# Seven products for eight in the mixer's input projection, with sums made by adding DMAs

## The chip, the cores and the metric

The kernel runs on one core of a Trainium2 chip. The metric is the device time of one execution in microseconds (us). Before the change three runs took 2020.88 to 2021.68 us, median 2021.68. Engines are named as in the profile: PE (TensorE, the matmuls), PEld (its weight loads), DVE (VectorE), ACT (ScalarE), POOL (GpSimd), SP (SyncE, which only issues DMAs here).

## The reference

One layer of a streaming encoder over T = 576 frames (512 of a prompt, 64 of a sample), width 1024, all in float32:

```
h = x + 0.5 * swiglu(rmsnorm(x), w_ffn1)          # 1024 -> 2 x 4096 -> 1024
h = h + mixer(rmsnorm(h))
h = h + 0.5 * swiglu(rmsnorm(h), w_ffn2);  y = rmsnorm(h)

mixer(u):  z, xbc, dt, aq, ak, av, mq, mk, mv, mo, mi, mf, gl = split(u @ w_in)
  y_ssd  = rmsnorm(ssd_scan(silu(conv4(xbc)), dt) * silu(z))      # 16 heads x 64, state 128
  y_att  = chunk-band softmax attention(aq, ak, av)               # 8 heads x 64
  y_ml   = rmsnorm(mlstm_scan(mq, mk, mv, mi, mf)) * sigmoid(mo)  # 4 heads x 128
  g_ssd, g_att, g_ml = split(sigmoid(gl))
  out = (g_ssd * (y_ssd @ w_proj_ssd) + g_att * (y_att @ w_proj_attn) + g_ml * (y_ml @ w_proj_mlstm)) @ w_out
```

Caches and states are inputs, and the new ones are outputs too. The input projection `u @ w_in` has 1024 rows and some 9,700 columns; it is the largest product of the mixer.

## The kernel before

Activations lie transposed in SBUF: 128 channels on the partitions, 8 channel slices, 576 frames along the free dimension. A float32 product is made from three fast ones: each operand is split into a rounded part (`wh`, `XH`, float32r, an ACT copy) and the rest (`wl`, `XL`, a DVE subtraction), and hi*hi + hi*lo + lo*hi are summed in PSUM.

A plain column tile (`gemm`, `matmuls`, L183) is 128 columns of a weight: a 512 KB load, one split of 128x1024 (L169, L170), and for each of the two frame ranges of 256 and 320 columns 8 slices x 3 = 24 matmuls. Its result goes through PSUM to `evac`, a DVE multiplication by the norm's factor `rs`.

The two FFNs already use another scheme for most of their first product (`swiglu_unit`, L404): two column tiles, two halves of the 1024 rows and two frame ranges of 288 form a 2x2 by 2x2 product, made in 7 products in place of 8 (`product`, L396, matmuls at L401). `operands` (L353) makes the seven moving operands `TH`, `TL` once per norm; `stationary` (L372) loads 1 MB of weights, adds them on POOL (L380 to L382) and splits seven blocks of 128x512. Each product is 4 x 3 = 12 matmuls of 288 columns. Three PSUM banks `pa`, `pb`, `pc` hold a unit.

The mixer runs twelve units in the order a0 a1 m0 a2 m1 m2 a3 m3 s0 s1 s2 s3 (a: two attention heads, 3 column tiles; m: one mLSTM head, 4 tiles; s: one SSD group of four heads, 6 tiles: z0, z1, B, C, x0, x1). Each unit's tiles are projected from `XH`, `XL`, and then the unit's own work runs on all engines: scores, softmax, transposes and products for attention (L616 to L689), `ml` (L708), the scan for SSD (`ssd`, L841 to L951). A `gate` tile feeds `gates` (L505), whose rows mLSTM and SSD need. Attention and mLSTM outputs are split into `YH`, `YL`; SSD outputs stay in `R1`.

`merge` (L954) then makes, for each of 4 column pairs, the sigmoid gates from `w_in`, the projections of attention and mLSTM, then the norm of the SSD outputs, the SSD gates and projection, and `w_out` (L1003 to L1010). The residual x waits in DRAM (`xs`) meanwhile.

Buffers are tiles from pools: a tag has a fixed number of buffers, and a new tile of a tag waits for the readers of the one whose place it takes; a pool opened after another was closed takes over its memory with the same kind of wait. In the mixer `g` (7) holds projected tiles, `t` (5) and `b` (6) a unit's larger temporaries, `P` (3) and `Q` (2) smaller ones. A planner places the program's instructions in each engine's queue by its own estimate of their times; each engine then works through its queue in order. SP issues nearly all DMAs, in the planner's order too.

## Time and profile before

| | us |
|---|---|
| median of three runs | 2021.68 |
| the profiled execution | 2022.94 |
| its span | 2021.2 |
| PE busy | 1968.9 |
| DVE busy | 1224.0 |
| ACT busy | 819.1 |
| POOL busy | 594.7 |

The profile is one execution. A row of groups gives line, engine, operation, tiles (out<-in), shapes and count, then total busy time in us, the mean in ns of one, and the idle time before with what ended it. A row of the timeline gives start and length in us. A row of stages gives a stretch, its length, busy time of PE, PEld, DVE, ACT and POOL with counts in brackets, the granted share of the PE clock, the share of DMA time and GB/s. Matmuls overlap, so that a row's duration is longer than the distance to the next.

In time the kernel runs FFN1 up to 608, the mixer's projections, attention and mLSTM up to about 950, SSD up to 1146, the merge and `w_out` up to 1415, then FFN2.

### The profile page before, as it was taken

To read this page: it belongs to the slowest core of one execution; us is meant where nothing else is said; L and a number is where in the kernel's file an instruction comes from. 1 tells how busy PE (TensorE), PEld (TensorE's weight loads), DVE (VectorE), ACT (ScalarE), POOL (GpSimd) and SP (SyncE) were. 2 spreads that over 40 slices of the span, in tenths; PEclk is the share of its full clock that TensorE was granted. 3 is DMA by queue.
4 is the path that set the end of the run, shared out by engine and by line. 5 is a ranking of instruction groups with operands and counts; after the bars stand their busy time and mean duration, and the time that the engine had idled before them with its cause. 6 is when DMAs were issued, how large, how long until landed. Compare 5 with 4: busy or idle time off the path is not lost.

```text
span 2021.2 us, 35535 instructions
## 1 busy us (share of the span) xinstructions
PE 1968.9 (97%) x14573; PEld 1916.4 (95%) x14573; DVE 1224.0 (61%) x2122; ACT 819.1 (41%) x1474; POOL 594.7 (29%) x564
## 2 busy tenths in 40 slices
PE   7899999999998999999999999999899999999997
PEld 7799999999997888989999999999799999999997
DVE  7865665656546856565777534444876566656554
ACT  3444334434433355454445323233453443344343
POOL 4443332433301010202343401330252343324221
PEclk8899999999998999999999999999899999999998
DMA  2221222232224322222333222321122213222221
GB/s 101 94 105 67 101 99 72 92 109 90 74 87 150 111 88 72 101 65 76 107 106 108 71 84 84 131 74 63 49 109 94 105 63 105 95 73 95 97 85 65
DMA packets 54778, 182.85 MB, mean 90 GB/s; under 512 B 5824, under 2 KB 17728, under 8 KB 47064
## 3 DMA queue, kind: packets, MB, share of 16 engines
q1 hardware_dynamic: 53640, 179.44, 25.5%
q8 instruction: 115, 1.88, 0.4%
q10 hardware_dynamic: 976, 1.14, 0.2%
q14 instruction: 47, 0.39, 0.1%
HBM read 171.80 MB, written 8.76 MB: 89 GB/s over the span
## 4 chain that ended last, share of the span: by engine, by line
PE 93%; DVE 3%; DMA 1%; issue 1%; POOL 1%; ACT 0%; POOLq 0%; SPq 0%; DVEq 0%; ACTq 0%
PE acc L183 55%; PE acc L401 31%; PE ps_s L652 1%; PE ps_v L663 1%; PE ps_x L640 1%; DMA w<-in_wblk 1%; PE ps_s L919 1%; PE ps_v L939 0%; DVE YL L261 0%; PE ps_x L945 0%; DVE YL L213 0%; PE ps_x L610 0%; DVE vl L213 0%; DVE TL L213 0%; DVE sq L297 0%
## 5 line engine op out<-in xcount | busy, mean ns | idle before, releaser
L183 PE MATMUL acc<-YH,wh 128*128 128x256 f32 (+1 forms) x1472 | 440.3, 300 | 14.4 <-ACT wh L169 14.4
L183 PE MATMUL acc<-YL,wh 128*128 128x256 f32 (+1 forms) x1472 | 440.2, 299 | 2.8 <-DVE YL L261 2.5
L183 PE MATMUL acc<-YH,wl 128*128 128x256 f32 (+1 forms) x1472 | 438.0, 300 | 3.7 <-DVE wl L170 3.7
L183 PE MATMUL acc<-XH,wh 128*128 128x256 f32 (+1 forms) x1360 | 407.9, 300 | 6.8 <-ACT wh L169 6.8
L183 PE MATMUL acc<-XH,wl 128*128 128x256 f32 (+1 forms) x1360 | 407.5, 300 | 2.5 <-DVE wl L170 2.5
L183 PE MATMUL acc<-XL,wh 128*128 128x256 f32 (+1 forms) x1360 | 408.8, 301 | 0.0
L169 ACT CAST wh<-w 128x1024 fp32r<-128x1024 f32 x177 | 185.6, 1048 | 292.3 <-PE acc L183 225.5
L183 PEld LDWEIGHTS acc<-YH,wh 128*128 128x128 f32 x1472 | 282.9, 192 | 15.2 <-ACT wh L169 15.0
L183 PEld LDWEIGHTS acc<-YL,wh 128*128 128x128 f32 x1472 | 283.7, 193 | 3.8 <-DVE YL L261 3.7
L183 PEld LDWEIGHTS acc<-YH,wl 128*128 128x128 f32 x1472 | 280.6, 192 | 5.4 <-DVE wl L170 5.2
L401 PE MATMUL acc<-TH,wh 128*128 128x288 f32 x928 | 274.2, 296 | 0.0
L401 PE MATMUL acc<-TL,wh 128*128 128x288 f32 x928 | 273.5, 295 | 0.0
L401 PE MATMUL acc<-TH,wl 128*128 128x288 f32 x928 | 271.6, 295 | 1.9 <-DVE wl L213 1.9
L183 PEld LDWEIGHTS acc<-XH,wh 128*128 128x128 f32 x1360 | 257.3, 189 | 13.7 <-ACT wh L169 7.4
L183 PEld LDWEIGHTS acc<-XH,wl 128*128 128x128 f32 x1360 | 257.1, 189 | 7.8 <-issue 4.7
L183 PEld LDWEIGHTS acc<-XL,wh 128*128 128x128 f32 x1360 | 257.4, 189 | 5.9 <-issue 5.4
L170 DVE TENSOR_TENSOR wl<-w,wh 128x1024 fp32r<-128x1024 f32 x177 | 224.5, 1269 | 61.2 <-ACT wh L169 61.2
L380 POOL TENSOR_TENSOR sm<-w 128x1024 f32<-128x1024 f32 x58 | 141.0, 2432 | 327.0 <-DVE vl L213 136.3
L401 PE MATMUL acc<-TH,vh 128*128 128x288 f32 x696 | 206.1, 296 | 1.7 <-ACT vh L212 1.7
L401 PE MATMUL acc<-TH,vl 128*128 128x288 f32 x696 | 205.3, 296 | 1.9 <-DVE vl L213 1.9
L401 PE MATMUL acc<-TL,vh 128*128 128x288 f32 x696 | 205.7, 296 | 0.0
L466 DVE SCALAR_TENSOR_TENSOR R<-acc,R 128x256 f32<-128x256 f32 (+1 forms) x256 | 115.1, 454 | 117.4 <-PE acc L183 116.2
(302 smaller groups left out, 3363.2 us busy)
## 6 DMA issues: line engine op xcount, KB each, us to landing
w<-in_wblk SPq DMA_DIRECT2D x177, 512.0 KB, 3.3
w<-in_sblk SPq DMA_DIRECT2D x58, 1024.0 KB, 4.9
b<-scr_rows SPq DMA_DIRECT2D x24, 288.0 KB, 4.2
b<-scr_rows SPq DMA_DIRECT2D x16, 144.0 KB, 3.3
R<-xs SPq DMA_DIRECT2D x1, 2304.0 KB
R<-in_xT SPq DMA_DIRECT2D x2, 640.0 KB, 7.9
xs<-R SPq DMA_DIRECT2D x4, 320.0 KB, 3.3
out_y<-R SPq DMA_DIRECT2D x2, 640.0 KB, 3.2
```

What stands on the lines that cost most here:

```text
L169: nc.scalar.copy(hi, w)
L170: nc.vector.tensor_tensor(lo, w, hi.bitcast(F32), op=ALU.subtract)
L183: nc.tensor.matmul(ps[:, :n], wt[:, wsl], xx[:, k0 + k, a:a + n], start=(k == 0 and i == 0), stop=(k == nk - 1 and i == 2))
L380: nc.gpsimd.tensor_tensor(s[:, 0:2, :], w[:, 0:2, :], w[:, 1:3, :], op=ALU.add)
L401: self.nc.tensor.matmul(ps, wt[:, wsl], xx[:, t, kk, :], start=(start and kk == 0 and i == 0), stop=(kk == 3 and i == 2), skip_group_check ...
L466: nc.vector.scalar_tensor_tensor(x[:, ot, sl], ps, 0.5, x[:, ot, sl], op0=ALU.mult, op1=ALU.add)
L640: nc.tensor.transpose(pt[:L, k:k + 128], P[:, k0 + k:k0 + k + L], self.ident)
L652: nc.tensor.matmul(ss[r][:, :nk], q[H[r], c * 128:(c + 1) * 128], kT[H[r], :nk], start=True, stop=True)
L663: nc.tensor.matmul(pv[H[r], c * 128:(c + 1) * 128], vt[:, k, H[r]], PT[r][:, k, :], start=(k == 0), stop=(k == c))
L919: nc.tensor.matmul(ps[:, :128], bt[:n, c, :], xw[:n, c, :], start=True, stop=True)
```

## The change

The mixer's 76 column tiles of `w_in` are regrouped. The six tiles of a0 and a1 and the gate tile stay plain. The other 70 become 35 pairs, each in seven products:

- `operands` is called four times during the plain tiles, so that `TH`, `TL` (now allocated for the whole kernel) hold the mixer's normalised input. They already contain `rs`, so that evacuations only scale.
- `pair` is the new unit: seven `product` calls, four ACT copies or activations from PSUM, three DVE evacuations, two of them with a sum.
- `stationary_fine` gets a pair's weights in pieces of 128x512: three loads (`wr`, 5 buffers), two sums made by DMA (`added`: a load on SP's queue into `wx`, 3 buffers, and a second DMA on POOL's queue that adds to it), and two sums made by POOL (`wy`, 2 buffers). Seven splits of 128x512 go to `ph`, `pl` (6 buffers). Plain tiles in the mixer are loaded and split in halves the same way.
- Three PSUM banks serve both forms in turn.

To make room, branch outputs go to DRAM (`ys`, 16 rows of 128x576) as they are made. `XH`, `XL` exist only for the plain tiles; `P`, `Q`, `t`, `bias` then take their memory, and after the last SSD unit `YH`, `YL` take it in turn, filled from `ys` by loads and splits. `b` is now six slices of `R1`; z of every SSD unit is in `R1` slices 0 and 1, and the unit's tile order is B, C, x0, x1, z0, z1. The squares for the SSD norm are summed at each unit's end. `merged` is `R1` itself, and `XH`, `XL` for `w_out` lie over `TH`, `TL`; x comes back by four DMAs after that. The order of units is a0 a1 m0 a2 a3 m1 m2 m3 s0 to s3; `g` has 8 buffers. In the FFN phases `YH`, `YL` move from the constant pool into the phase's own pool, and the squares of the first norm share one buffer.

The core of the diff:

```diff
-NB = 177
-NS = 58
+NB = 107
+NS = 93
-BUFS = {"g": 7, "b": 6, "t": 5, "P": 3, "Q": 2}
+BUFS = {"g": 8, "t": 5, "P": 3, "Q": 2}
...
+    def stationary_fine(self, src):
+        nc = self.nc
+        def load(q):
+            w = self.ring("wr")
+            nc.sync.dma_start(w, src[:, q, :])
+            return w
+        def added(q0, q1):
+            x = self.ring("wx")
+            nc.sync.dma_start(x, src[:, q0, :])
+            nc.gpsimd.dma_start(x, src[:, q1, :], accum_op=ALU.add)
+            return x
+        out = {}
+        x1 = added(0, 1)
+        a11, a22 = load(0), load(2)
+        x3 = self.ring("wy")
+        nc.gpsimd.tensor_tensor(x3, x1, a22, op=ALU.add)
+        out[self.T_X1] = self.parts(x1)
+        out[self.T_A11] = self.parts(a11)
+        a21 = load(3)
+        x2 = added(1, 2)
+        x4 = self.ring("wy")
+        nc.gpsimd.tensor_tensor(x4, x3, a21, op=ALU.add)
...
+    def pair(self, one, two):
...
+        self.product(pa, ops, self.T_X1, True)
+        v = tmp()
+        nc.scalar.activation(v, pa, AF.Copy, scale=s1)
+        self.product(pb, ops, self.T_A11, True)
+        put1(1, H[1], emit(pb, s1, v, ALU.add))
+        self.product(pa, ops, self.T_X3, False)
+        u = tmp()
+        nc.scalar.activation(u, pa, AF.Copy, scale=s2)
+        self.product(pc, ops, self.T_X4, True)
+        m6 = tmp()
+        nc.scalar.activation(m6, pc, AF.Copy, scale=s2)
+        self.product(pa, ops, self.T_A22, False)
+        put2(0, H[0], emit(pa, -s2, m6, ALU.add))
+        self.product(pc, ops, self.T_A21, False)
+        put2(1, H[1], emit(pc, s2, u, ALU.subtract))
+        self.product(pa, ops, self.T_X2, False)
+        put1(0, H[0], emit(pa, s1))
...
-        self.split(y, self.YH[:, i, :], self.YL[:, i, :])
+        nc.sync.dma_start(self.ys[i], y)
...
+        gates(O_GA, 0)
+        gates(O_GM, 0)
+        with self.pools("my", "yp"):
+            self.YH = self.yp.tile([128, 8, T], F32R, name="YH")
...
+            for i in range(8):
+                self.split(load(i), self.YH[:, i, :], self.YL[:, i, :])
...
+                tiles = [t for u in ORDER[:2] for t in got[u][0]]
+                self.plain(tiles[:3], half_major=True)
+                for n, t in enumerate(tiles[3:]):
+                    self.operands(x, self.rs, C_GM, n)
+                    self.plain([t])
+                self.operands(x, self.rs, C_GM, 3)
```

## The prediction

> **What bounds the kernel now.** I read the page's first part, then the chain of waits, then the matmuls in order of time, then the busy time by stages.

> ```profile
> span 2021.2 us, 35535 instructions
> PE 1968.9 (97%) x14573; PEld 1916.4 (95%) x14573; DVE 1224.0 (61%) x2122; ACT 819.1 (41%) x1474; POOL 594.7 (29%) x564
> PE 93%; DVE 3%; DMA 1%; issue 1%; POOL 1%; ACT 0%; POOLq 0%; SPq 0%; DVEq 0%; ACTq 0%
> ```

> PE sets the end: 93% of the chain. Its busy time says nothing of the price of one matmul, since neighbours overlap; that is the distance between starts:

> ```profile
> 304.98 0.30 PE L401 MATMUL acc<-TH,wh 128*128 128x288 f32 x1
> 306.58 0.30 PE L401 MATMUL acc<-TH,vh 128*128 128x288 f32 x1
> ...
> 1204.82 0.28 PE L183 MATMUL acc<-XH,wh 128*128 128x256 f32 x1
> 1207.65 0.31 PE L183 MATMUL acc<-XH,wh 128*128 128x320 f32 x1
> 1208.38 0.31 PE L183 MATMUL acc<-XH,wl 128*128 128x320 f32 x1
> ```

> Twelve matmuls of 288 columns take 1.60 us (0.1333 each), 24 of 256 take 2.83 (0.118), five of 320 take 0.73 (0.146). A plain column tile, 24 + 24 matmuls, costs PE 24 x 0.118 + 24 x 0.146 = 6.33 us; two cost 12.66. A unit of seven products is 84 matmuls of 288: 11.20 us.

> Stages: plain tiles at the mixer's start; attention and mLSTM; three ssd units; the ssd tail; merge; w_out; the start of FFN2.

> ```profile
> 613.70:664.00 50.30, 46.14 (x314) 43.95 (x315) 32.16 (x64) 16.11 (x29) 6.54 (x13) 0.89 0.33 116
> 664.00:958.00 294.00, 294.00 (x2136) 259.71 (x2135) 179.48 (x453) 138.18 (x313) 39.74 (x83) 1.00 0.26 85
> 958.00:1110.00 152.00, 152.00 (x1188) 145.63 (x1187) 113.47 (x279) 68.94 (x133) 61.63 (x108) 1.00 0.34 110
> 1110.00:1146.00 36.00, 36.00 (x290) 34.33 (x291) 20.61 (x47) 9.88 (x17) 18.40 (x23) 1.00 0.21 71
> 1146.00:1366.00 220.00, 220.00 (x1660) 219.78 (x1660) 101.07 (x157) 68.25 (x117) 45.49 (x49) 1.00 0.27 93
> 1416.00:1485.00 69.00, 57.09 (x373) 54.51 (x374) 56.07 (x75) 30.12 (x46) 22.69 (x15) 0.90 0.21 77
> ```

> Columns: length, then PE, PEld, DVE, ACT and POOL busy, the granted clock, the DMA share. PE has no hole from 664 to 1366; DVE is at 61% in attention and mLSTM, 75% in ssd, 46% in the merge. So time saved on PE counts, until DVE, which pays for the new scheme, has no room.

> **The change, part by part.**

> *Saving.* 70 column tiles become 35 pairs: 35 x (12.66 - 11.20) = **-51.1 us** on PE. All else is what this sets loose.

> *What a pair asks of the other engines.*

> ```profile
> L170 DVE TENSOR_TENSOR wl<-w,wh 128x1024 fp32r<-128x1024 f32 x177 | 224.5, 1269 | 61.2 <-ACT wh L169 61.2
> L213 DVE TENSOR_TENSOR vl<-w,vh 128x512 fp32r<-128x512 f32 x58 | 61.4, 1059 | 1.0
> L212 ACT CAST vh<-sm 128x512 fp32r<-128x512 f32 x116 | 72.3, 623 | 160.1 <-POOL sm L380 155.3 <-PE acc L401 4.8
> L420 ACT COPY P<-acc 128x288 f32<-128x288 f32 x58 | 22.8, 393 | 2.2 <-PE acc L401 2.2
> L427 DVE TENSOR_TENSOR P<-P,acc 128x288 f32<-128x288 f32 x58 | 26.3, 453 | 122.4 <-PE acc L401 122.3
> L699 DVE SCALAR_TENSOR_TENSOR g<-acc,rs 128x320 f32<-128x320 f32 x16 | 7.8, 486 | 6.5 <-PE acc L183 6.4
> L811 DVE TENSOR_TENSOR P<-acc,rs 128x256 f32<-128x256 f32 x16 | 6.7, 416 | 1.4 <-PE acc L183 1.4
> L213 DVE TENSOR_TENSOR YL<-g,YH 128x576 fp32r<-128x576 f32 x68 | 57.8, 850 | 13.3 <-ACT YH L212 13.1
> L223 DVE TENSOR_TENSOR na<-na,sq 128x256 f32<-128x256 f32 x27 | 12.0, 444 | 2.9 <-ACT sq L222 2.2
> ...
> 305.70 0.69 DVE L213 TENSOR_TENSOR vl<-w,vh 128x512 fp32r<-128x512 f32 x1
> ...
> 314.63 1.23 DVE L213 TENSOR_TENSOR vl<-sm,vh 128x512 fp32r<-128x512 f32 x1
> ...
> 314.01 1.29 POOL L381 TENSOR_TENSOR sm<-sm,w 128x512 f32<-128x512 f32 x1
> ```

> Two plain tiles cost DVE 2 x 1.27 (splits) + 2 x (0.42 + 0.49) (evacuations) = 4.36 us. A pair costs 7 splits of 512 and 3 evacuations of 288: 7 x 0.69 + 3 x 0.45 = 6.2 us with POOL still, and 7 x 1.06 + 1.4 = 8.8 at the mean of the second row. The last two rows show why: the split at 314.63 begins while a POOL add runs (314.01 to 315.30) and takes 1.23 for 0.69. Each pair brings two POOL adds of 512 and two DMAs issued by POOL. [...]

> *ssd.* A unit takes 152/3 = 50.7 us: DVE 37.8, ACT 23.0, POOL 20.5. DVE loses 6 x 1.27 of splits and about 6.0 of evacuations, and gains 21 x 0.69 = 14.5, twelve or so evacuations (4.6, the conv's being in pieces) and four adds of squares (1.8): +7.3, less about 1 for the 0.06 by which neighbours overlap. Six adds of 1.3 us on POOL, met half the time at half their length or more, give about +3. DVE: 47. ACT: 23 + 21 x 0.62 - 6 x 1.05 + 12 x 0.39 + 1.7 = 36. PE: 50.7 - 3 x 1.46 = 46.3. Two engines are full; neither packs perfectly in order, so I take 48: four units, **+7** above the PE figure. Bounds: 0, and at 1.06 a split 37.8 - 13.6 + 22.3 + 6.4 = 52.9, or +26.

> *Attention and mLSTM.* Eleven pairs bring DVE 11 x about 3 us, less the eight splits of outputs that move to the merge (0.85 each): 179.5 + 26 in 294 - 16 = 278, 74%. No price for that; the merge (12 pairs in 220 us) has more room still.

> *Operands of the pairs.* Four calls in the plain stage, at the rows of the FFN's:

> ```profile
> L359 DVE SCALAR_TENSOR_TENSOR xk<-R,cst,rs 128x576 f32<-128x576 f32 x16 | 14.1, 925 | 3.0 <-ACT rs L277 3.0
> L363 DVE TENSOR_TENSOR xd<-xk 128x576 f32<-128x576 f32 x8 | 7.2, 902 | 0.1
> L213 DVE TENSOR_TENSOR TL<-xd,TH 128x1440 fp32r<-128x1440 f32 x8 | 13.2, 1653 | 1.7 <-ACT TH L212 1.7
> L213 DVE TENSOR_TENSOR TL<-xk,TH 128x576 fp32r<-128x576 f32 x8 | 5.9, 749 | 0.0
> ```

> 2 x 0.93 + 2.5 x 0.9 + 1.65 + 0.75 = 6.5, four times 26 us. DVE's 32.2 becomes 58 in 50.3; some of the 32.2 belongs to attention, which now comes later. **+5** before the first pair; bounds 0 and 12.

> *Attention starts later.* P, Q, t lie where XH and XL were, so unit a0 waits for the gate tile's last matmul, about 664:

> ```profile
> 649.54 0.60 PE L610 MATMUL ps_x<-ident,g 128*128 128x128 f32 x4
> ...
> 704.03 0.23 DVE L688 COPY t<-ps_v 128x64 f32<-128x64 f32 x1 [0.74 <-PE ps_v L687]
> ```

> It took 54 us, under which PE had plain tiles. Now a0 and a1 hold six of the eight g buffers, and one m0 pair (11.2 us) fits before a0 returns some. **+8**, nearer to the low end because vT and q are freed well before the unit ends; bounds 0 and 25 (40 us of attention less that pair and its own matmuls).

> *The ssd tail.* The projections need YH and YL, which now lie on the branch buffers and come back from DRAM once ssd(3) is through:

> ```profile
> 1103.71 0.80 DVE L822 SCALAR_TENSOR_TENSOR g<-P,cst,g 128x579 f32<-128x579 f32 x1
> ...
> 1145.31 0.30 POOL L951 TENSOR_TENSOR R<-g,R 128x64 f32<-128x64 f32 x1
> ```

> 41 us from the last conv to the end, and some 6 for squares, their total and four split slices: 47. Cover on PE: the z pair (now last) 11.2, two gate pairs 22.4, ssd's own matmuls 50.7 - 6 x 6.33 = 12.7: 46. **+4**; bounds 0 and 15 (the z pair, whose R1 slots unit s2 frees late, as cover for nothing).

> *Ends of the mixer.* FFN's YH and YL move into its pool, on top of the mixer's weight rings, so their norm can't run beside the last w_out matmuls, and the mixer's first weights wait for FFN1's:

> ```profile
> 613.72 0.58 PE L183 MATMUL acc<-XH,wh 128*128 128x256 f32 x1 [5.18 <-ACT wh L169]
> ...
> 1419.79 0.74 PE L237 MATMUL ps_x<-ones,na 128*128 128x1 f32 x4 [4.57 <-DVE na L223]
> ```

> Both places stand idle about 5 us already. **+5** for FFN2 (eight adds and splits of 0.44 and 0.5 are 7.5; bounds 0 and 9), **+2** for FFN1's end and the shared squares buffer at the start (0 and 6).

> *Sums by DMA.* A pair's X1 is a load and an adding load behind it. No row has an adding DMA; the nearest are

> ```profile
> w<-in_wblk SPq DMA_DIRECT2D x177, 512.0 KB, 3.3
> w<-in_sblk SPq DMA_DIRECT2D x58, 1024.0 KB, 4.9
> ```

> so 6.6 to 10 us for both, against three buffers for two sums per pair, 1.5 pairs or 17 us ahead. POOL waits for the first to land before it issues the second, and the x3 add is queued behind. **+2**; bounds 0 and 35 x 1.5 = 52 (a POOL add of 1.5 ahead of each).

> Sum: -51.1 + 7 + 5 + 8 + 4 + 5 + 2 + 2 = -18.1. The profiled execution took 2022.94 (its span 2021.2 and 1.7 around it): 2004.8. The median of the runs, 2021.68, lies 1.3 below: **2003.5 us**.

> **The rivals.**

> *DVE becomes the bound (slower).* Place: attention to ssd; price: splits at 1.06 behind POOL's adds. ssd +26 for +7; 77 splits of 0.37 more in attention, half of it on the path, +14; a0, chained through the same queue, at its bound, +17. 2003.5 + 50 = 2053. It decides against the change once an ssd unit passes 50.7. For: the 1059 row. Against: 61% and 46% around it, and FFN units that run without holes at that mean.

> *PE stays full (faster).* The planner fills every hole but the ends: -51.1 + 9 = -42, 1980. For: no hole from 664 to 1366 now. Against: the g buffers.

> *The pairs don't cost 11.2 (no gain).* X1 late behind POOL, 0.7 us a pair: +25 less the 2 above, 2026. For: POOL's 20 of 50 us in ssd. Against: the 17 us ahead.

> *Holes halve the clock.* Holes of 5.18, 1.67 and 2.48 us stand before the 613.70 row's 0.89, and 0.90 stands at 1416; 11% of 50 us is 5.5 lost, beyond the hole. Three new holes (a0, hand-over, tail) at 3.5: +10, 2013.5. [...]

> **How the numbers follow.** Forecast 0.36, DVE bound 0.26, PE full 0.17, no gain 0.11, clock 0.10. 0.2% (4 us) is about what a measurement can tell from no change. Faster: 0.33 + 0.17 + 0.09 + 0.03 = 0.62; slower: 0.23 + 0.06 + 0.01 = 0.30; same: 0.08. The forecast's own range is 1990 to 2018. The range for 8 in 10 takes in the no-gain case, half of the full-PE case and half of the DVE case: 1982 to 2046.

> **What would show it.** Starts of 288-column matmuls 0.133 apart in the mixer; a unit of ssd near 48 us with DVE above 90%; a PE hole around 670 to 700 ended by attention, another before the first projection ended by DVE YL. Wrong if those holes are absent, if waits on the splits stand between products throughout, or if X1's products wait for DMA.

## The result and the profile after

The changed kernel takes **2075.65 us** (median of four runs, 2073.32 to 2079.95) against 2021.68 (2020.88 to 2021.98) on the same chip: **1.027 times** the time before, 95% interval 1.0252 to 1.0288. The forecast was 2003.5, its range ended at 2046.

The first part of the changed kernel's profile page and its chain of waits:

```profile
span 2074.2 us, 36310 instructions
PE 1945.8 (94%) x14153; PEld 1879.2 (91%) x14153; DVE 1358.7 (66%) x2361; ACT 944.4 (46%) x1843; POOL 783.4 (38%) x704
PE 81%; DVE 8%; DMA 4%; ACT 3%; issue 2%; POOL 2%; SPq 0%; POOLq 0%; DVEq 0%; ACTq 0%
```

PE still leads the chain, but with 81% for 93%. The span grew by 53.0. PE's *busy* time fell by 23.1 (1968.9 to 1945.8) and its *idle* time rose by 76.1 (52.3 to 128.4).

Did a pair cost what the forecast said? The first and the last of twelve consecutive matmuls of a pair, in the timeline of the changed kernel:

```profile
1131.12 0.30 PE L543 MATMUL acc<-TH,ph 128*128 128x288 f32 x1
...
1132.56 0.30 PE L543 MATMUL acc<-TH,pl 128*128 128x288 f32 x1
```

Eleven distances in 1.44 us: 0.131 each, and 420 matmuls fewer in all. The 51.1 us are saved where PE runs at full rate. So about 28 of them came back as slower matmuls (51.1 less 23.1), and 76.1 us went into holes. Both have a place in the stages. Before, first, with the three last ssd units as the third row, and then after; columns as in the prediction:

```profile
0.00:600.00 600.00, 580.25 (x4251) 576.48 (x4252) 373.29 (x527) 245.12 (x409) 215.72 (x157) 0.98 0.26 91
600.00:664.00 64.00, 54.68 (x373) 52.23 (x372) 39.51 (x87) 21.38 (x40) 6.54 (x13) 0.89 0.39 133
998.00:1146.00 148.00, 148.00 (x1163) 141.94 (x1162) 104.87 (x254) 66.20 (x124) 61.38 (x99) 1.00 0.30 99
1366.00:1420.00 54.00, 49.43 (x373) 49.17 (x371) 25.82 (x48) 19.78 (x37) 0.00 (x0) 1.00 0.15 50
1420.00:1540.00 120.00, 111.88 (x787) 109.30 (x787) 88.89 (x115) 54.82 (x87) 44.46 (x29) 0.94 0.23 82
```

```profile
0.00:600.00 600.00, 578.00 (x4254) 574.15 (x4255) 376.29 (x543) 241.42 (x407) 218.10 (x153) 0.97 0.26 91
600.00:677.00 77.00, 59.82 (x422) 58.30 (x420) 57.90 (x124) 35.29 (x74) 12.44 (x20) 0.91 0.40 125
677.00:988.00 311.00, 292.67 (x1964) 248.36 (x1965) 227.43 (x532) 178.75 (x452) 127.48 (x161) 0.95 0.49 129
988.00:1178.00 190.00, 161.66 (x1187) 149.30 (x1187) 158.40 (x346) 108.99 (x230) 120.46 (x151) 0.93 0.53 138
1028.00:1178.00 150.00, 128.20 (x936) 119.58 (x937) 125.81 (x271) 88.86 (x186) 91.40 (x114) 0.93 0.52 137
1178.00:1204.00 26.00, 17.60 (x109) 16.77 (x108) 16.21 (x27) 11.70 (x21) 9.18 (x10) 0.74 0.55 167
1204.00:1414.00 210.00, 207.09 (x1545) 206.34 (x1544) 125.15 (x195) 97.37 (x194) 82.84 (x81) 0.99 0.50 138
1464.00:1590.00 126.00, 106.59 (x751) 104.52 (x752) 96.70 (x149) 65.62 (x120) 44.23 (x28) 0.91 0.22 76
```

Length less PE busy is the hole time of a stage:

| stage | PE idle before | after | more |
|---|---|---|---|
| FFN1 to 600 | 19.8 | 22.0 | 2.2 |
| plain tiles and hand-over | 9.3 | 17.2 | 7.9 |
| attention and mLSTM | 0 | 18.3 | 18.3 |
| ssd | 0 | 28.3 | 28.3 |
| up to the first projection | 0 | 8.4 | 8.4 |
| merge | 0 | 2.9 | 2.9 |
| `w_out` and the start of FFN2 | 12.7 | 20.3 | 7.6 |

(Before, PE was busy for the whole of 664 to 1366, as the prediction's rows show. `w_out` after, 1414 to 1464, has 0.9 of the 20.3.) The granted clock was 1.00 throughout the middle before; now it is 0.95, 0.93 and 0.74 in the third, fourth and sixth row. The busy time of each of these times what is missing from 1.00 is 14.6 + 11.3 + 4.6 = 30.5 us, which is where the 28 are.

Three ssd units take 150 us for 148: DVE's share there went from 71% to 84%, PE's from 100% to 85%. The change gave PE less work, and PE waited instead. The holes that stand in one piece:

```profile
676.86 0.61 PE L543 MATMUL acc<-TH,ph 128*128 128x288 f32 x1 [8.11 <-ACT ph L254]
...
1140.88 0.69 PE L1013 MATMUL ps_x<-ident,g 128*128 128x128 f32 x2 [6.32 <-ACT t L729]
...
1190.68 0.58 PE L226 MATMUL acc<-YH,ph 128*128 128x256 f32 x1 [5.73 <-ACT ph L254]
...
1471.85 0.58 PE L226 MATMUL acc<-YH,wh 128*128 128x256 f32 x1 [8.73 <-ACT wh L254]
```

They are the first pair's first product, a transpose in the last ssd unit, the first projection, and FFN2's first tile. Together they are 28.9 us of 128.4: most of the idle time is in many shorter waits.

### The profile page after: what moved, and what is told of

It is laid out like the page before. It is cut to its first block, busy times and chain, and to the rows that moved or that the text cites. A ratio compares the mean times of both kernels' runs of the same rounds, so it can differ in the third digit from the quotient of the medians.

```text
span 2074.2 us, 36310 instructions
## 1 busy us (share of the span) xinstructions
PE 1945.8 (94%) x14153; PEld 1879.2 (91%) x14153; DVE 1358.7 (66%) x2361; ACT 944.4 (46%) x1843; POOL 783.4 (38%) x704
## 3 DMA queue, kind: packets, MB, share of 16 engines
q1 hardware_dynamic: 78264, 198.06, 28.9%
## 4 chain that ended last, share of the span: by engine, by line
PE 81%; DVE 8%; DMA 4%; ACT 3%; issue 2%; POOL 2%; SPq 0%; POOLq 0%; DVEq 0%; ACTq 0%
PE acc L543 45%; PE acc L226 31%; DMA R<-scr_rows 2%; DVE pl L255 1%; PE ps_s L784 1%; PE ps_v L795 1%; DVE YL L305 1%; PE ps_x L772 1%; DVE TL L255 1%; DVE R L1029 1%; ACT ph L254 0%; DVE wl L255 0%; DVE xk L411 0%; DMA w<-in_wblk 0%; DVE YL L255 0%
## 5 line engine op out<-in xcount | busy, mean ns | idle before, releaser
L226 PE MATMUL acc<-YH,wh 128*128 128x320 f32 (+1 forms) x1216 | 363.0, 302 | 27.2 <-ACT wh L254 26.5
L226 PE MATMUL acc<-YL,wh 128*128 128x320 f32 (+1 forms) x1216 | 364.2, 301 | 3.0 <-DVE YL L305 2.8
L226 PE MATMUL acc<-YH,wl 128*128 128x256 f32 (+1 forms) x1216 | 360.5, 300 | 5.4 <-DVE wl L255 5.4
L543 PE MATMUL acc<-TH,ph 128*128 128x288 f32 x980 | 303.4, 311 | 23.9 <-ACT ph L254 9.0
L543 PE MATMUL acc<-TH,pl 128*128 128x288 f32 x980 | 297.1, 306 | 3.4 <-DVE pl L255 3.4
L543 PE MATMUL acc<-TL,ph 128*128 128x288 f32 x980 | 295.5, 302 | 0.0
L543 PEld LDWEIGHTS acc<-TH,ph 128*128 128x128 f32 x980 | 189.5, 194 | 36.8 <-ACT ph L254 9.9
L543 PEld LDWEIGHTS acc<-TH,pl 128*128 128x128 f32 x980 | 188.9, 193 | 9.9 <-issue 4.7
L543 PEld LDWEIGHTS acc<-TL,ph 128*128 128x128 f32 x980 | 191.6, 196 | 2.9 <-issue 2.4
L543 PEld LDWEIGHTS acc<-TL,wh 128*128 128x128 f32 x928 | 176.5, 190 | 0.0
## 6 DMA issues: line engine op xcount, KB each, us to landing
w<-in_sblk SPq DMA_DIRECT2D x58, 1024.0 KB, 4.8
w<-in_wblk SPq DMA_DIRECT2D x76, 512.0 KB, 3.3
```

Of the source, the lines that this page charges most:

```text
L226: nc.tensor.matmul(ps[:, :n], wt[:, wsl], xx[:, k0 + k, a:a + n], start=(k == 0 and i == 0), stop=(k == nk - 1 and i == 2))
L543: self.nc.tensor.matmul(ps, wt[:, wsl], xx[:, t, kk, :], start=(start and kk == 0 and i == 0), stop=(kk == 3 and i == 2), skip_group_check ...
```

## The experiments

The first theory was: VectorE (DVE) is what the freed time runs into, in attention and ssd. Rivals: the adding DMAs; GpSimd's (POOL's) adds, beside which a split took 1.23 us for 0.69 in the prediction's rows; buffers. All times below stand against the changed kernel's 2075.65; its own runs spread over 6.6 us, so that a single run within some 4 us of it says no change. The kernel before took 2021.25 to 2023.21 beside them. Unless said otherwise an experiment is one run. The planner places the instructions of every kernel anew, so that the queues of two kernels can differ in more than the edit; the two experiments that change buffers alone moved the time by -0.3 and +3.9.

### Five of a pair's seven subtractions left out

```diff
-        out[self.T_X3] = self.parts(x3)
...
+        lo = out[self.T_A11][1]
+        for name, src2 in ((self.T_X3, x3), (self.T_X4, x4), (self.T_A22, a22), (self.T_A21, a21), (self.T_X2, x2)):
+            hi = self.wp.tile([128, 512], F32R, name="ph", tag="ph", bufs=self.bufs["wp"])
+            nc.scalar.copy(hi, src2)
+            out[name] = (hi, lo)
```

> Left out: in every pair five of the seven DVE subtractions; the matmuls of X3, X4, A22, A21 and X2 read A11's rest in their place, so PE, ACT, POOL and the DMAs do all that they did. Theory (DVE is what holds PE up between the hand-over and the end of ssd): 175 splits of 0.84 us leave DVE, 147 us in all, about 95 of them before the merge, and the time falls by 40 us or more, to 2035 or less. Rival (the adding DMAs and POOL's queue come late): less than 15 us. Rival (buffers: two z slots, eight g, set the pace): less than 15 us.

Measured: 2035.43, 40.2 less. DVE's busy time fell by 132.4 (to 1226.3, level with before), PE's idle time by 22.6 (to 105.8) and its busy time by 17.9 with the same matmuls:

```profile
span 2033.7 us, 36015 instructions
PE 1927.9 (95%) x14153; PEld 1866.4 (92%) x14153; DVE 1226.3 (60%) x2186; ACT 947.8 (47%) x1847; POOL 751.9 (37%) x704
```

DVE's load is the largest of the causes that were tried. But with DVE no busier than before, the kernel is still 12.8 slower than the 2022.62 beside it: something else eats the rest.

### The adding DMAs, GpSimd's adds, and the operands' buffers

Three kernels, one edit each (in the second, X3 and X4 are then split from X1's and A21's blocks):

```diff
-            nc.gpsimd.dma_start(x, src[:, q1, :], accum_op=ALU.add)
...
-        x3 = self.ring("wy")
-        nc.gpsimd.tensor_tensor(x3, x1, a22, op=ALU.add)
-        x4 = self.ring("wy")
-        nc.gpsimd.tensor_tensor(x4, x3, a21, op=ALU.add)
...
+        out[self.T_X3] = self.parts(x1)
+        out[self.T_X4] = self.parts(a21)
...
-            d1, d2, d3 = ring("wx"), ring("wx"), ring("wx")[:, 0:1, :]
+            d1, d2, d3 = ring("wx"), ring("wy"), ring("wy")[:, 0:1, :]
```

> Left out: the second DMA of X1 and X2 (70 adding DMAs on POOL's queue), so that those two blocks are loaded, not summed. Theory (DVE): at most 15 us, through fewer late first products; 2060 to 2075. Rival (adding DMAs late, POOL held): 30 us or more, 2045 or less, and no holes ended by the split of a first block.

Measured: 2060.59, 15.1 less, at the far end of the first range and half of what the rival asked for. DVE's busy time fell by 4.3 only (to 1354.4), so this price is not DVE's load. The DMA issues of the changed kernel show the price of a sum in two steps, 2.9 and 4.7 us from issue to landing one behind the other; and POOL stood 70.5 us in front of its issues until the base load had landed (group row of POOL, line 464):

```profile
wx<-in_sblk SPq DMA_DIRECT2D x70, 256.0 KB, 2.9
wx<-in_sblk POOLq DMA_DIRECT2D x70, 256.0 KB, 4.7
```

```profile
L464 POOL DMA_DIRECT2D wx<-in_sblk x70 | 63.4, 929 | 219.3 <-DMA wx<-in_sblk 70.5 <-DVE sm L762 19.4 <-DVE t L732 17.8
```

Each issue holds POOL 0.93 us, too.

> Left out: the two POOL additions of each pair; X3 and X4 are split from X1's and A21's blocks. DVE has the same number of splits. [...] If POOL's queue is what is late: 20 us or more with splits still at 0.8.

Measured: 2068.12, 7.5 less. The adds do cost DVE time: with the same 2361 instructions DVE is busy 31.1 us less (1327.6), and the splits of attention and ssd take 0.74 and 0.77 us where the changed kernel's take 0.83 to 0.85. The groups of DVE between 677 and 1178, changed kernel first, then this run:

```profile
L255 DVE TENSOR_TENSOR pl<-wr,ph 128x512 fp32r<-128x512 f32 x75 | 62.8, 841 | 9.1 <-ACT ph L254 8.9
L255 DVE TENSOR_TENSOR pl<-wx,ph 128x512 fp32r<-128x512 f32 x50 | 42.4, 850 | 12.3 <-ACT ph L254 11.6
L255 DVE TENSOR_TENSOR pl<-wy,ph 128x512 fp32r<-128x512 f32 x50 | 41.3, 827 | 7.5 <-ACT ph L254 5.8 <-PE acc L543 0.7 <-ACT r L901 0.6
```

```profile
L255 DVE TENSOR_TENSOR pl<-wr,ph 128x512 fp32r<-128x512 f32 x100 | 73.7, 740 | 17.4 <-ACT ph L254 16.7
L255 DVE TENSOR_TENSOR pl<-wx,ph 128x512 fp32r<-128x512 f32 x74 | 57.2, 773 | 30.1 <-ACT ph L254 29.2 <-PE acc L539 0.3
```

So the splits are shorter without the adds, which goes with the prediction's two rows (0.69 alone, 1.23 beside an add); but 31 us of DVE bought 7.5 us of time, less than the 10 to 25 that the author had estimated.

> The operands' differences take one buffer of wx and the two of wy in place of all three of wx, so that the first pair's sums can be loaded before the last operands are split. Nothing is left out. Theory: the hole of 8.1 us before the first pair's first product shrinks to 3 or less, and the time falls by 5 to 9 us, since nothing behind it depends on that place. If the stages behind are paced by DVE alone, DVE's queue still holds the same work and less than 4 us is gained.

Measured: 2075.32, no change. The 8.11 us hole before the first product shrank to 1.76, and a hole of 2.65 appeared further on, ended by DVE's split. In the timeline of this run:

```profile
670.08 0.40 PE L543 MATMUL acc<-TH,ph 128*128 128x288 f32 x1 [1.76 <-ACT ph L254]
...
684.77 0.40 PE L543 MATMUL acc<-TH,pl 128*128 128x288 f32 x1 [2.65 <-DVE pl L255]
```

The first product starts almost 7 us earlier and nothing is won: what sets attention's pace is not there. Attention itself did not start earlier: DVE's first step on its scores (line 788) is at 679.40 here and at 676.77 in the changed kernel.

### All three relieved

The edits of the first three kernels together.

> The changed kernel without five of a pair's seven subtractions on VectorE, without the adding DMAs and without the two adds on GpSimd (left out: the low parts and the sums of the weights, so the projections' values are not the reference's; the products on TensorE are all there). If the three are separate prices, the reliefs of the single runs add: 2035.4 - 15 - 7.5 = about 2013, range 2005 to 2019. If they are three doors to one and the same wait (VectorE's queue), little comes on top of the first: 2027 to 2035. If work beside TensorE were all that eats the saving, the time falls to the saving and the ends alone: 2022.9 - 51 + 7 + 8 = about 1987.

Measured: 2019.16, 56.5 less, just above the range that ended at 2019: the single reliefs (40.2, 15.1, 7.5) nearly add up. It is 4.1 below the kernel before beside it (2023.21), where the plan had 51 less the ends.

```profile
span 2017.5 us, 35655 instructions
PE 1924.8 (95%) x14153; PEld 1865.2 (92%) x14153; DVE 1200.1 (59%) x2186; ACT 943.6 (47%) x1845; POOL 601.4 (30%) x564
```

PE is idle for 92.7, 40 more than before, and busy for 44.1 less. So even with DVE, POOL and the adding DMAs relieved, four fifths of the saving goes into holes. By the stages of this run, worked out as in the table above, they lie in ssd (14.0), in front of the first projection (8.4), before FFN2 (6.6), in attention and mLSTM (6.2), in the hand-over (3.7) and in the merge (1.2).

Two rivals for this rest stand untested. ACT's load stayed: it is busy for 943.6 us here and for 819.1 in the kernel before, and no run took that off. And a pair's seven products share three PSUM banks: of PE's holes in ssd, 10.0 of the changed kernel's 28.3 us end, as the profile infers it, when ACT or DVE has emptied such a bank (`uv`, `P`, `R` in `pair`), 9.0 of the 18.3 with fewer splits, and 5.3 of the 14.0 here. No run gave the pairs a fourth bank.

### The first sums on GpSimd in place of the adding DMAs

```diff
-            nc.sync.dma_start(x, src[:, q0, :])
-            nc.gpsimd.dma_start(x, src[:, q1, :], accum_op=ALU.add)
+            nc.gpsimd.tensor_tensor(x, w4[q0], w4[q1], op=ALU.add)
...
+        w4 = {q: load(q) for q in (0, 1, 2)}
...
```

> The changed kernel with the first sums added on GpSimd from the loaded blocks, no adding DMA: 70 more adds of some 1.5 us on GpSimd (+105), 70 issues of 0.93 fewer (-65), and VectorE's splits meet an add more often. If VectorE behind GpSimd's adds is what costs, slower than the changed kernel: 2085 to 2110. If the adding DMAs (their issue and their landing) are the dear part, faster: 2055 to 2068. Between 2068 and 2085 the choice of the adder does not matter.

Measured: 2093.14, 17.5 more; DVE is busy 33 us longer (1391.7). The adding DMAs cost 15, but the sum that they replace would have cost twice that: this part of the change is a good choice in a dear scheme.

### Two sets of z slots

```diff
-        return self.R1[:, 2 + (self.b_i - 1) % 6, :]
+        i = (self.b_i - 1) % 6
+        if i < 4:
+            return self.R1[:, 4 + i, :]
+        return self.fp.tile([128, T], F32, name="b", tag="b", bufs=2)
...
-            return ("w_in", col), 1.0, lambda h, sl, emit: emit(self.R1[:, j, sl])
+            return ("w_in", col), 1.0, lambda h, sl, emit: emit(self.R1[:, 2 * (g % 2) + j, sl])
...
```

> The changed kernel with two sets of slots for the z tiles (and the broadcast rows moved to four other slots and two small new buffers), so that unit s2's z pair need not wait until s0 or s1 has given its slots back. If VectorE is the bound of the ssd stage, no change: 2071 to 2080. If the single z slots hold the stage (the 78 us between the ends of s1 and s2 beside 34 between s0 and s1), faster by 8 or more: 2067 or less, and the units' ends lie evenly.

Measured: 2079.55, no change. The distances between the ends of s0 to s3 (POOL's last product of each unit) went from 35, 77, 38 to 53, 57, 27, so the slots did shape the order; they did not set the length.

### The kernel before with its splits done twice

```diff
-        nc.vector.tensor_tensor(lo, w, hi.bitcast(F32), op=ALU.subtract)
+        for _ in range(2 if desc[0] == "w_in" else 1):
+            nc.vector.tensor_tensor(lo, w, hi.bitcast(F32), op=ALU.subtract)
```

> The kernel before, with the split's subtraction of each w_in weight block done twice on VectorE (same result): 76 x 1.27 = +97 us of VectorE, about the +112 us that the pairs brought to the same stages, and TensorE's work, the buffers and the order of the units as they were. If VectorE's load is what costs, this alone slows it at the rate that the run with fewer splits gave (40 of 147 us: 0.27), to about 2049, range 2035 to 2065. If the cost lies in where attention, the z pair and the projections now start, it stays within 5 us: 2018 to 2028.

Measured: 2036.51 against 2023.21, 13.3 more. So DVE's load alone, with PE's work and the buffers as they were, costs time in a kernel whose DVE was busy for 61%:

```profile
PE 1970.5 (97%) x14573; PEld 1915.3 (94%) x14573; DVE 1308.7 (64%) x2198; ACT 818.9 (40%) x1474; POOL 622.1 (31%) x564
```

But 84.7 us of DVE for 13.3 is 0.16 each, for the 0.27 that I had carried over. Attention and mLSTM, then ssd, in this run:

```profile
664.00:955.00 291.00, 289.69 (x2098) 254.37 (x2097) 207.01 (x481) 127.42 (x303) 43.09 (x81) 1.00 0.27 86
955.00:1164.00 209.00, 200.62 (x1550) 190.59 (x1549) 165.52 (x355) 90.23 (x162) 100.26 (x134) 0.99 0.30 96
```

The same in the kernel before:

```profile
664.00:945.00 281.00, 281.00 (x2036) 246.90 (x2035) 171.03 (x439) 129.31 (x301) 37.37 (x77) 1.00 0.26 86
945.00:1146.00 201.00, 201.00 (x1577) 192.77 (x1576) 142.53 (x339) 87.69 (x161) 82.41 (x137) 1.00 0.30 99
```

So 36 us more of DVE made 1.3 us of holes in attention and mLSTM, and 23 us more made 8.4 in ssd; the merge has none. In attention, DVE's added work made PE wait hardly at all while PE had its whole work to cover it; in ssd it did.

### Idle matmuls in the holes

```diff
+    def fill(self, x, n, after):
+        ps = self.ps("x")
+        with self.tc.issue_after(after):
+            for _ in range(n):
+                self.last_mm = self.nc.tensor.matmul(ps[:, :256], x[:, 0:128], x, start=True, stop=True).ins
...
+            self.fill(self.TH[:, 0, 0, 0:256], 55, self.last_mm)
...
+                    self.fill(self.TH[:, 0, 0, 0:256], 8, self.total([acc], n, pt))
...
+                self.fill(self.TH[:, 0, 0, 0:256], 45, self.last_spread)
...
+            self.fill(self.TH[:, 0, 0, 0:256], 60, self.last_mm)
```

> The changed kernel with idle matmuls (256 columns each, into a bank that nobody reads; same result) put where TensorE stands still: 55 behind the last plain tile, 8 behind each total of squares and 45 behind the spread before the first projection, 60 before FFN2's first tile. If a hole's half clock behind it is a price of its own, the half-rate stretches there (6.8, 13.7 and 10.2 us) go, half of 30.7 us is won less what the idle matmuls delay: 2060 to 2068. If the work behind the holes waits for VectorE anyway, TensorE's rate does not matter there: 2071 to 2078.

Measured: 2066.4, 9.3 less, inside the range of the clock's price. The mean granted clock rose from 0.963 to 0.978; between 600 and 1600 the stretches at half rate add up to 58 us, where the changed kernel has 113 and the kernel before 27. But the gain does not lie where the idle matmuls stand. In this run ssd, the 26 us around the first projection, and FFN2's start:

```profile
987.00:1169.00 182.00, 154.47 (x1111) 140.43 (x1109) 151.95 (x332) 104.28 (x222) 113.87 (x145) 0.94 0.51 138
1169.00:1195.00 26.00, 25.29 (x197) 24.87 (x196) 16.01 (x29) 12.29 (x23) 8.15 (x9) 1.00 0.61 177
1454.00:1580.00 126.00, 111.98 (x800) 108.96 (x799) 96.17 (x148) 65.94 (x122) 44.24 (x28) 0.95 0.22 76
```

Around the first projection the clock is 1.00 for 0.74, and at FFN2's start 0.95 for 0.91; but from ssd's end to FFN2's first product it is 293 us in both kernels, and 602 from there to the end. So filling these holes won nothing, be it that PE's rate does not matter there or that the idle matmuls delay as much as they win. Attention and mLSTM end 0.8 us earlier than in the changed kernel. Nearly all of the gain is in ssd, 182 us for 190, where no idle matmul was put and where the instructions run in another order. What won it there stays open.

The same in the kernel before, with 45 idle matmuls ahead of FFN2:

```diff
+            self.fill(self.YH[:, 7, 320:576], 45, self.last_mm)
             rs = self.norm(x, C_G2, self.YH, self.YL)
```

> The kernel before with 45 idle matmuls before FFN2's first tile, where it stands idle 4.57 us (same result). By the clock's price the 120 us behind run at full rate instead of 0.94: 2 to 5 us faster, 0.998 to 0.999 of the time. If the first total, which comes behind the idle matmuls, is what is late, no change or 1 us slower.

Measured: 0.9992 of the time before, interval 0.9983 to 1.0001. From 1416 to 1485 the granted clock is 0.95 for 0.90: about 7 of the 13.7 us at half rate there are gone, but a gain is not settled.

### Fewer splits in one stage at a time

The first experiment's edit, for the pairs of one stage alone (`if few:` around it).

> The changed kernel with five of a pair's seven subtractions left out in the 12 pairs of the ssd units alone (their low parts are left out of the products' operands). All 35 pairs together gave 40. If the price lies in ssd, as the forecast had it (ssd +26 at the dear end of its bounds), 18 to 28 faster: 2048 to 2058. If attention is where it lies, less than 10: 2066 or more.

> The same for the 11 pairs of attention and mLSTM alone, for which the forecast set no price. If DVE at 74% on average hides them there, less than 5: 2071 or more. If the chains of attention wait in VectorE's queue behind the splits (93% busy from 668 to 737), 10 to 20: 2056 to 2066. The two stages together should give 30 to 40, the 12 pairs of the merge nothing.

Measured: 2061.59 with the 12 pairs of ssd (14.1 less, where 18 or more was expected) and 2055.99 with the 11 pairs of attention and mLSTM (19.7 less). What the first experiment's 40.2 leave, 6.5, is the 12 pairs of the merge, if the three add; as what three single runs leave, it may as well be nothing.

| where | DVE busy less | time less | per us of DVE |
|---|---|---|---|
| attention and mLSTM | 41.7 | 19.7 | 0.47 |
| ssd | 37.3 | 14.1 | 0.38 |
| merge (the rest) | 53.4 | 6.5 | 0.12 |

Attention and mLSTM in the run without their splits, to set beside the 677 row above:

```profile
677.00:969.00 292.00, 279.51 (x1953) 240.04 (x1953) 186.57 (x471) 182.06 (x454) 125.48 (x161) 0.99 0.52 136
```

Holes went from 18.3 to 12.5, and those of them that end with DVE from 10.8 to 6.2. The clock went from 0.95 to 0.99 with them: most of this stage's half rate was gone together with short waits behind DVE's splits.

## Why the prediction was wrong

**The saving** was right: 0.131 per matmul for 0.133, 84 matmuls a pair.

**The step that failed** is "Attention and mLSTM". DVE's share was forecast well: 74% of the stage, and the row of 677 to 988 has 227.4 in 311, 73%; but the load (227 for 206) and the stage (311 for 278) were both larger. What was wrong is the sentence behind it, "No price for that". The splits of the 11 pairs alone cost 19.7 us there. A stage's mean share of an engine says what is left over if its work can be done at any time; here scores, softmax and transposes stand in DVE's queue behind splits, and PE has 16 us less of its own to do meanwhile. One such place, in DVE's timeline of the changed kernel:

```profile
732.89 0.88 DVE L255 TENSOR_TENSOR pl<-wr,ph 128x512 fp32r<-128x512 f32 x1
733.70 0.69 DVE L255 TENSOR_TENSOR pl<-wx,ph 128x512 fp32r<-128x512 f32 x1
734.32 0.27 DVE L775 COPY Q<-ps_x 64x128 f32<-64x128 f32 x1
```

Two splits run ahead of the copy that empties a transpose's PSUM tile, and PE stands still for 0.88 us until that copy is through (the row of its next transpose, at 734.74, stands in the last section). Of PE's 18 us of waits in the stage, 10.8 end with DVE. The 61% and 46% that the prediction held against its DVE rival were read in the same way. For the merge, where DVE splits and evacuates and little waits behind, the reading fits (0.12 or less).

The ends of the stages say the same. The last mLSTM unit ended at 988 for 948, where the terms up to there (+2, +5, +8, and PE's 16 less) leave it within 1 us of where it was: that is 41 us of the error of 72. Some 3 lie in the four ssd units, and 27 between ssd's end and FFN2's first product (293 us for 275, forecast 266).

**ssd, +7.** The unit was put at 48 with DVE busy for 47. Measured from s0's end: 50.0 (150 for three units, which took 35, 77 and 38), DVE busy for 41.9. From the end of the last mLSTM unit it is 190 for four, 47.7 each. So the time was about right, and the reason for it was not: "two engines are full" described no engine. PE's work that had run under ssd moved behind it: the first projection began 35 us ahead of ssd's end before, and begins 12 us behind it now. Of the 28.3 us of holes, leaving out the splits gave back 14.1 in time, and 14.0 us of holes remain when DVE, POOL and the adding DMAs are all relieved; z slots are not their cause. What they are was not separated: the waits for a pair's PSUM banks are the largest part that the profile names. That the units' chains now have 33.6 us of pairs as cover for 38.0 of plain tiles fits too, but is only argued.

**The clock, 0 in the sum.** As a rival it had three holes and 10 us. Its 3.5 us a hole was an estimate that no run shows; between 600 and 1600 the changed kernel has fifteen stretches of 3.4 to 13.7 us at half rate, 113 us together, where the kernel before has three, 27 us together. About 28 us of PE's busy time came back through them. That is a size, not yet a price in time: where the idle matmuls brought the clock back, around the first projection (1.00 for 0.74) and at FFN2's start (0.95 for 0.91), no time was won. The second step that failed is in "How the numbers follow": the clock stood beside the other cases as an alternative with a chance of its own, though each of them makes holes. The DVE rival's 2053 and 28 more would have been 2081; that this comes close is luck, since the parts of that rival were off on both sides.

**Sums by DMA, +2** (0 to 52) came to 15; how much of it is a late first product of a pair and how much is POOL's time was not separated.

**The ends** were the right places at somewhat larger sizes: hand-over 7.9 of idle time for 5, FFN1 2.2 for 2, the tail 8.4 of idle time and 4.6 of clock for 4, FFN2 with `w_out` 7.6 for 5. The prediction's waits were there: a hole at 676.86, one before the first projection. The hand-over's releaser was another one than thought, since the operands' temporaries lay in the `wx` buffers that X1 needs; but it did not matter. **Attention later, +8:** a0 ended at 737 for 704. DVE's first step on its scores came at 676.8, where the kernel before has 651.0: 26 us later. No run started attention earlier with the rest as it is, so what this term cost is open.

**The rivals.** "DVE becomes the bound" had the sign, the places and the mechanism, at 0.26; its split price of 1.06 was too high (0.84), its 26 for ssd was too high as well (14), its 14 for attention too low (20). "PE stays full" rested on "no hole from 664 to 1366", which says that there was enough cover, not how much of it was needed.

## What to carry to other kernels

When PE has no holes, its own work is the cover for chains through the other engines, and a change that takes PE work away takes cover away: price added DVE work by whether the stage is chained through DVE (here 0.4 to 0.5 us of time for each us) or streams (0.1 or less), not by DVE's mean share. Attention shows both sides: 36 us more of DVE made 1.3 us of holes when PE had its whole work, and the 42 us of five splits a pair cost 19.7 when it had less. Holes and slower matmuls came together here, 76.1 us of the one and about 28 of the other, and belong into every case together. A scheme that saves 51 us of PE for 113 us of DVE (from the first pair to `w_out`) is worth trying first where the other engines stream; here that is the merge, which was not tried alone.

## What the runs showed of the hardware

**Here the clock was halved without a long hole, too.** In the kernel before, 13.7 us at half rate begin at 611.2, within the hole of 5.18 us, and 6.8 us at 1420.1, just behind the one of 4.57. Here are the stages around one half-rate stretch in attention of the changed kernel:

```profile
728.10:731.50 3.40, 3.40 (x30) 2.79 (x29) 3.37 (x9) 3.14 (x9) 2.33 (x2) 1.00 0.72 141
731.50:734.90 3.40, 1.58 (x9) 0.98 (x9) 3.02 (x6) 1.69 (x4) 3.30 (x4) 1.00 0.61 188
734.90:738.30 3.40, 3.40 (x26) 2.10 (x25) 2.05 (x10) 0.92 (x4) 0.40 (x3) 0.50 0.87 213
738.30:748.60 10.30, 10.14 (x30) 6.41 (x31) 5.30 (x19) 6.10 (x23) 0.91 (x1) 0.50 0.80 252
748.60:752.00 3.40, 3.40 (x21) 2.33 (x19) 1.49 (x3) 0.72 (x3) 0.00 (x0) 1.00 0.22 65
```

From 731.5 to 734.9 PE was busy for 1.58 of 3.4 us, and the waits that the timeline names there are short:

```profile
733.12 0.74 PE L772 MATMUL ps_x<-ident,P 128*128 128x128 f32 x5 [0.94 <-DVE P L763]
734.74 0.33 PE L698 MATMUL ps_x<-ident,R 128*128 128x128 f32 x1 [0.88 <-DVE Q L775]
```
